# The passes with the low halves of the weights moved to the end of their bank, in a three-layer transformer kernel

## The chip, the cores and the metric

The kernel runs on one core of one Trainium2 chip. The metric is device time of one execution in microseconds (us); the kernel before takes 881.45 us, the median of three runs between 879.95 and 884.21. The engines have short names in all rows below: PE is TensorE (PEld its weight loads), DVE is VectorE, ACT is ScalarE, POOL is GpSimd, and SP is SyncE, whose queue (SPq) issues the DMA transfers.

## What is computed

256 tokens of width 1024 pass through three blocks, each modulated by a vector worked out from a condition `c` (`h = rmsnorm(x) * (1 + scale) + shift`, and a gate on the way back):

```
block 1: z = h @ w_in ; split into q_lat, kv_lat, k_rope, conv_in, gates
         q = rmsnorm(q_lat) @ w_uq ; kv = rmsnorm(kv_lat) @ w_ukv ; rope ; causal attention @ w_o_attn
         conv = silu(layernorm(causal depthwise conv, 31 taps, of a gated half)) @ w_conv_out
         x += gate1 * ((g_attn * attn + g_conv * conv) @ w_out)
         x += gate2 * mixture of experts(h2), 4 groups x 8 experts, 2 experts of one group per token
layer A: gated delta rule: 4-tap conv on q, k, v ; chunks of 64 tokens, a triangular inverse in each ;
         state scan over the chunks ; rmsnorm(o) * silu(z) @ a_w_out
layer B: forgetting attention: 16 heads of 64, decay from a cumulated log gate ; * silu(z) @ b_w_out
```

All inputs and outputs are fp32.

## The kernel before, in words

**One weight product.** [...] The activation is split into a high and a low half once per block (`split`: `h_hi` or `h4h` on ACT, `h_lo` or `h4l` on DVE, L700 and L703). Each weight piece (1 MB: 1024 rows by 256 columns, or another shape of that size) is split when it arrives (`wpieces`): the transfer fills a tile `raw` (4 buffers, from SP's queue), ACT writes the high half into a tile `hl` (L309), and `lo = raw - hi` goes into a second tile `hl` (L313). The four `hl` tiles hold two pieces. A piece is split in two halves of 128x1024 (k 0 to 3 and k 4 to 7): for the first half `lo` runs on DVE, for the second on POOL (both on POOL in a short stretch of layer A). Both engines do nothing else for that time, and everything queued behind on them waits.

**A job.** A product of one piece is a `Job`: its `load` part issues the transfer and yields the split steps, its `body` part issues 48 matmuls into one PSUM bank (2 halves of the output by 8 k by 3 passes): high weight by high activation, high weight by low activation, low weight by high activation. What they are called depends on which operand is loaded into the array:

- `gemm_feat_g` (the weight is loaded, output transposed): L483, L484, and L485 with the low half of the weight
- `gemm_tok_g` (the activation is loaded): L351, L352 with the low half of the weight, L353
- `gemm_wide`: L391, L392 (low half), L393
- `gemm_tok_m`: L424, L425 (low half), L426
- `gemm_parts`: the last product of the kernel, which has the same three passes and is not touched

The body yields after every dozen or so matmuls with its estimated cost. A feeder (`Feed`) uses these yields: it issues split steps of the next jobs, transposes, the condition products (L530, with the sums at L563 and L587 and the DVE steps L589 and L590 behind them), and pieces of the side work (the convolution's taps L1050, attention). So the order of instructions on each engine is set when the program is written out, by these yields; on the chip every engine runs its own list in order and waits at semaphores.

**Where it stands.** Block 1 runs to 284 us (attention and the convolution beside the weight products of `w_in`, then `w_o_attn`, `w_conv_out`, `w_out`), the experts to 390 us, layer A to 705 us, layer B to 884 us.

Of the kernel before, what the change touches and what calls it, by code (L numbers as in the profile page):

```python
# [179 lines left out]
class Kern:  # L180
# [146 lines left out]
    def gemm_tok_g(self, h, ko, w2d, n0, n, evac, psum=None):  # L327

        st = {}

        def load():
            st["pc"], todo = self.wpieces(w2d, 0, ko, n0, n)
            return todo

        def body():
            nc, pieces = self.nc, st["pc"]
            hh, hl = h
            if n <= 256:
                p = self.pmm()
                pts = [p[:, :n], p[:, 256:256 + n]]  # L340
                order = [(t, pc) for t in range(2) for pc in pieces]
            else:
                pts = [(psum or self.pmm)()[:, :n] for _ in range(2)]
                order = [(t, pc) for pc in pieces for t in range(2)]
            cost = 0.0
            for t, (k0, kn, whi, wlo) in order:
                for k in range(kn):
                    kk = k0 + k
                    a = hh[:, kk, t * 128:(t + 1) * 128]
                    b = hl[:, kk, t * 128:(t + 1) * 128]  # L350
                    nc.tensor.matmul(pts[t], a, whi[:, k, :], start=kk == 0, stop=False)  # L351
                    nc.tensor.matmul(pts[t], a, wlo[:, k, :], start=False, stop=False)  # L352
                    nc.tensor.matmul(pts[t], b, whi[:, k, :], start=False, stop=kk == ko - 1)  # L353
                    cost += 3 * n / 2400.0
                    if cost > 1.2:
                        yield cost
                        cost = 0.0
            with self.tc.high_priority(offset=self.LEAD):
                if n <= 256:
                    evac(p.rearrange("p (t n) -> p t n", t=2)[:, :, :n])  # L360
                else:
                    for t in range(2):
                        evac(t, pts[t])
            yield cost

        return Job(load, body)

    def gemm_wide(self, h, ko, w2d, n0, evac, n=256, step=8):

        pts = []  # L370

        def make(ka, kb):
            st = {}

            def load():
                st["pc"], todo = self.wpieces(w2d, ka, kb, n0, n)
                return todo

            def body():
                nc = self.nc  # L380
                if ka == 0:
                    pts.extend([self.pmm()[:, :n], self.ptp()[:, :n]])
                hh, hl = h
                (k0, kn, whi, wlo), = st["pc"]
                cost = 0.0
                for t in range(2):
                    for k in range(kn):
                        kk = k0 + k
                        a = hh[:, kk, t * 128:(t + 1) * 128]
                        b = hl[:, kk, t * 128:(t + 1) * 128]  # L390
                        nc.tensor.matmul(pts[t], a, whi[:, k, :], start=kk == 0, stop=False)  # L391
                        nc.tensor.matmul(pts[t], a, wlo[:, k, :], start=False, stop=False)  # L392
                        nc.tensor.matmul(pts[t], b, whi[:, k, :], start=False, stop=kk == ko - 1)  # L393
                        cost += 3 * n / 2400.0
                        if cost > 1.2:
                            yield cost
                            cost = 0.0
                    if kb == ko:
                        evac(t, pts[t])
                yield cost  # L400

            return Job(load, body)

        return [make(k, min(k + step, ko)) for k in range(0, ko, step)]

    def gemm_tok_m(self, h, ko, w2d, n0, n, evac, i0, hl=None):

        st = {}

        def load():  # L410
            st["pc"], todo = self.wpieces(w2d, 0, ko, n0, n, hl)
            return todo

        def body():
            (_, _, whi, wlo), = st["pc"]
            hh, hl_ = h
            for i in range(n // 256):
                p = self.pmm().rearrange("p (t n) -> p t n", t=2)
                sl = slice(256 * i, 256 * i + 256)
                for t in range(2):  # L420
                    for k in range(ko):
                        a, b = [o[:, k, t * 128:(t + 1) * 128] for o in (hh, hl_)]
                        mm = self.nc.tensor.matmul
                        mm(p[:, t], a, whi[:, k, sl], start=k == 0, stop=False)  # L424
                        mm(p[:, t], a, wlo[:, k, sl], start=False, stop=False)  # L425
                        mm(p[:, t], b, whi[:, k, sl], start=False, stop=k == ko - 1)  # L426
                evac(i0 + i, p)
                yield 0.64 * ko

        return Job(load, body)  # L430
# [32 lines left out]
    def gemm_feat_g(self, h, ko, w2d, n0, n, evac):  # L463

        st = {}

        def load():
            st["pc"], todo = self.wpieces(w2d, 0, ko, n0, n)
            return todo

        def body():
            nc, pieces = self.nc, st["pc"]
            hh, hl = h
            cost = 0.0
            for bp in range(n // 256):
                p = self.pmm().rearrange("p (b t) -> p b t", b=2)
                for b in range(2):
                    c0 = bp * 256 + b * 128
                    for k0, kn, whi, wlo in pieces:
                        for k in range(kn):  # L480
                            kk = k0 + k
                            wa, wb = whi[:, k, c0:c0 + 128], wlo[:, k, c0:c0 + 128]
                            nc.tensor.matmul(p[:, b, :], wa, hh[:, kk, :], start=kk == 0, stop=False)  # L483
                            nc.tensor.matmul(p[:, b, :], wa, hl[:, kk, :], start=False, stop=False)  # L484
                            nc.tensor.matmul(p[:, b, :], wb, hh[:, kk, :], start=False, stop=kk == ko - 1)  # L485
                            cost += 0.32
                            if cost > 1.2:
                                yield cost
                                cost = 0.0
                with self.tc.high_priority(offset=self.LEAD):  # L490
                    evac(bp, p)
            yield cost

        return Job(load, body)


# [2275 lines left out]
```

## Time and profile before

| | |
|---|---|
| median of three runs | 881.45 us (879.95 to 884.21) |
| the profiled execution | 885.71 us |
| its span on the core | 883.8 us |
| mean granted clock of TensorE | 0.96 of full |
| PE busy | 781.9 us, 88% of the span, 6583 matmuls |
| DVE busy | 580.1 us, 66% |
| ACT busy | 394.7 us, 45% |
| POOL busy | 284.1 us, 32% |
| memory read | 187.91 MB, 214 GB/s over the span |

The profile is of one execution, 4.3 us longer than the median of the three timed runs; 1.9 us of its time lie outside the span. Busy shares are means over stages with different limits. The rows further down come from five views: the page's summary; the list of waits, by the line that waits and what released it; the chain of work that ended last, followed back from the end; the timeline of one engine, with the idle time before an instruction and its releaser in brackets; and a table by windows of time. In names such as `hl<-raw,hl` the written tile comes first, then those read.

### The profile page before, as it was taken

The numbers are of one execution on the slowest core, as the hardware profiler recorded it, in microseconds if no ns is written. First come the engines' busy times: TensorE is split into PE (matmuls) and PEld (weight loads), VectorE is DVE, ScalarE is ACT, GpSimd is POOL, SyncE is SP. The second block draws the span as 40 slices with busy tenths as digits, with TensorE's granted clock in tenths as the row PEclk, the third lists the DMA queues.
The fourth block names the chain that finished last, engine by engine and source line by source line (L and its number), as shares of the span: only waits on it lengthen the run. The fifth ranks groups of instructions, "written<-read, shape, count | busy, mean of one in ns | idle before, by whom it ended". The sixth has DMA issues, their size and how long they took to land.

```text
span 883.8 us, 16485 instructions
## 1 busy us (share of the span) xinstructions
PE 781.9 (88%) x6583; PEld 677.2 (77%) x6583; DVE 580.1 (66%) x1167; ACT 394.7 (45%) x734; POOL 284.1 (32%) x217
## 2 busy tenths in 40 slices
PE   3779797889998899969889797998999998999996
PEld 1568676677987655538789696898998887999986
DVE  1587866675665854548778988477756466577555
ACT  2355424345544232237574235454454463554552
POOL 0144212212333200003552264134553443545433
PEclk9899999999999999999899898899999998999999
DMA  8886675777999699996444285363348643454201
GB/s 284 290 250 216 209 237 189 259 260 264 371 402 372 248 409 407 409 379 201 135 154 128 88 269 187 101 188 96 112 151 301 198 150 108 132 148 139 96 25 48
DMA packets 126325, 190.25 MB, mean 215 GB/s; under 512 B 11242, under 2 KB 84184, under 8 KB 126244
## 3 DMA queue, kind: packets, MB, share of 16 engines
q1 hardware_dynamic: 123764, 185.78, 61.0%
q10 hardware_dynamic: 1984, 1.79, 0.6%
q0 software_dynamic: 496, 1.59, 0.5%
q8 instruction: 53, 0.87, 0.4%
q14 instruction: 28, 0.23, 0.1%
HBM read 187.91 MB, written 1.22 MB: 214 GB/s over the span
## 4 chain that ended last, share of the span: by engine, by line
PE 45%; DVE 24%; DMA 15%; ACT 6%; issue 5%; POOL 3%; SPq 1%; ACTq 0%; POOLq 0%; DVEq 0%
DMA ew<-in_expert_w_up_dram 6%; DMA raw<-in_w_in_dram 6%; PE mm L351 4%; PE mm L353 4%; PE mm L352 4%; PE mm L483 3%; DVE hl L313 3%; PE mm L485 3%; PE mm L484 3%; DVE cacc L2035 2%; DVE tp L1050 2%; POOL hl L313 2%; PE mm L530 2%; ACT hl L309 2%; DMA ew<-in_expert_w_down_dram 1%
## 5 line engine op out<-in xcount | busy, mean ns | idle before, releaser
L313 POOL TENSOR_TENSOR hl<-raw,hl 128x1024 fp32r<-128x1024 f32 (+3 forms) x82 | 192.5, 2349 | 325.0 <-ACT hl L309 300.8
L309 ACT ACTIVATE hl<-raw 128x1024 fp32r<-128x1024 f32 (+4 forms) x156 | 153.7, 1018 | 50.0 <-DMA raw<-in_w_in_dram 31.1
L313 DVE TENSOR_TENSOR hl<-raw,hl 128x1024 fp32r<-128x1024 f32 (+2 forms) x74 | 99.2, 1340 | 73.0 <-ACT hl L309 72.6
L483 PE MATMUL mm<-h_hi,hl 128*128 128x256 f32 x448 | 134.4, 300 | 5.5 <-DVE b L589 2.5
L485 PE MATMUL mm<-h_hi,hl 128*128 128x256 f32 x448 | 128.8, 288 | 7.7 <-POOL hl L313 4.0
L484 PE MATMUL mm<-h_lo,hl 128*128 128x256 f32 x448 | 128.2, 286 | 0.3 <-DVE h_lo L703 0.2
L483 PEld LDWEIGHTS mm<-h_hi,hl 128*128 128x128 f32 x448 | 87.5, 195 | 10.9 <-ACT hl L309 4.1
L485 PEld LDWEIGHTS mm<-h_hi,hl 128*128 128x128 f32 x448 | 87.6, 196 | 9.5 <-POOL hl L313 5.3
L484 PEld LDWEIGHTS mm<-h_lo,hl 128*128 128x128 f32 x448 | 87.8, 196 | 1.0 <-DVE h_lo L703 0.9
L351 PE MATMUL mm<-hl,h4h 128*128 128x256 f32 (+1 forms) x256 | 76.3, 298 | 1.1 <-ACT h4h L700 0.7
L352 PE MATMUL mm<-hl,h4h 128*128 128x256 f32 (+1 forms) x256 | 72.6, 283 | 0.8 <-DVE hl L313 0.5
L353 PE MATMUL mm<-hl,h4l 128*128 128x256 f32 (+1 forms) x256 | 72.8, 284 | 0.4 <-DVE h4l L703 0.2
L1050 DVE SCALAR_TENSOR_TENSOR tp<-uq,convw,tp 128x256 f32<-128x256 f32 x120 | 58.5, 487 | 3.1
L351 PEld LDWEIGHTS mm<-hl,h4h 128*128 128x128 f32 x256 | 49.1, 192 | 2.8 <-ACT h4h L700 0.9
L352 PEld LDWEIGHTS mm<-hl,h4h 128*128 128x128 f32 x256 | 49.1, 192 | 1.2 <-DVE hl L313 0.7
L353 PEld LDWEIGHTS mm<-hl,h4l 128*128 128x128 f32 x256 | 48.8, 191 | 1.0 <-DVE h4l L703 1.0
L2035 DVE SCALAR_TENSOR_TENSOR cacc<-mm,aconv,cacc 128x255 f32<-128x255 f32 (+2 forms) x96 | 38.7, 472 | 14.0 <-ACT cacc L2032 14.0
L1332 PE MATMUL tp<-ew,xs 128*32 128x256 f32 x528 | 37.7, 379 | 4.5 <-DMA ew<-in_expert_w_up_dram 4.5
L351 PE MATMUL mm<-hl,h_hi 128*128 128x256 f32 x128 | 38.4, 300 | 0.0
L1332 PEld LDWEIGHTS tp<-ew,xs 128*32 128x32 f32 x528 | 23.1, 110 | 20.0 <-issue 9.3
L352 PE MATMUL mm<-hl,h_hi 128*128 128x256 f32 x128 | 36.4, 284 | 0.0
L353 PE MATMUL mm<-hl,h_lo 128*128 128x256 f32 x128 | 36.3, 283 | 0.0
(679 smaller groups left out, 1997.4 us busy)
## 6 DMA issues: line engine op xcount, KB each, us to landing
raw<-in_ada_w_dram SPq DMA_DIRECT2D x30, 1024.0 KB
raw<-in_a_w_in_dram SPq DMA_DIRECT2D x24, 1024.0 KB
ew<-in_expert_w_gate_dram SPq DMA_DIRECT2D x32, 512.0 KB
ew<-in_expert_w_up_dram SPq DMA_DIRECT2D x32, 512.0 KB
ew<-in_expert_w_down_dram SPq DMA_DIRECT2D x16, 1024.0 KB
raw<-in_b_w_in_dram SPq DMA_DIRECT2D x15, 1024.0 KB
raw<-in_w_in_dram SPq DMA_DIRECT2D x12, 1024.0 KB
raw<-in_a_w_out_dram SPq DMA_DIRECT2D x8, 1024.0 KB
```

What stands on the lines that cost most here:

```text
L309: nc.scalar.activation(pc[2][:, ks], v[:, ks], AF.Copy)
L313: eng.tensor_tensor(pc[3][:, ks], v[:, ks], pc[2][:, ks].bitcast(F), OP.subtract)
L351: nc.tensor.matmul(pts[t], a, whi[:, k, :], start=kk == 0, stop=False)
L352: nc.tensor.matmul(pts[t], a, wlo[:, k, :], start=False, stop=False)
L353: nc.tensor.matmul(pts[t], b, whi[:, k, :], start=False, stop=kk == ko - 1)
L483: nc.tensor.matmul(p[:, b, :], wa, hh[:, kk, :], start=kk == 0, stop=False)
L484: nc.tensor.matmul(p[:, b, :], wa, hl[:, kk, :], start=False, stop=False)
L485: nc.tensor.matmul(p[:, b, :], wb, hh[:, kk, :], start=False, stop=kk == ko - 1)
L530: nc.tensor.matmul(p[32 * g:32 * g + 32, :], crep[:, hf * 4 + g, :], raws[hf][:, g, :], start=hf == 0, stop=hf == 1)
L1050: nc.vector.scalar_tensor_tensor(dst, u[:, b, tp:tp + 256], w(b, tp), dst, op0=OP.mult, op1=OP.add)
L1332: nc.tensor.matmul(pg[32 * s:32 * s + 32, :], xs[:, k, c0 + 32 * s:c0 + 32 * s + 32], gu[s][:, :, k * 128:(k + 1) * 128], start=k == 0, st ...
L2035: nc.vector.scalar_tensor_tensor(acc[:, b, sh:], p[:, b, 0:256 - sh], w(b, 3 - sh), acc[:, b, sh:], op0=OP.mult, op1=OP.add)
```

## The change

In the four functions named above the passes that use the low half of the weight are issued after all passes with the high half, for both halves of the output. A bank now takes 32 matmuls with the high half (high and low activation in turn), then 16 with the low half. The count of matmuls, their operands and their weight loads stay as they are. The bank is cleared once (`start` on its first matmul only) and closed once, because the two output halves are now both open at the same time. `gemm_wide` hands over its first bank only when the low passes of that bank are through, eight matmuls before the end of the job, where it used to do so at the job's half. The cost that a matmul reports to the feeder is nearly the same, so the yields come again after about a dozen matmuls. Lines behind the changed functions move by 10 (L687 is L697 in the new numbering, L587 is L597, L530 is L540, L600 is L610, L1116 is L1126); in the changed functions L483, L484, L485 become L494, L495, L492, and L351, L352, L353 become L356, L353, L357.

```diff
 # gemm_feat_g (gemm_tok_g, gemm_wide and gemm_tok_m are rewritten in the same way)
-                for b in range(2):
+                for late, b in ((0, 0), (0, 1), (1, 0), (1, 1)):
                     c0 = bp * 256 + b * 128
                     for k0, kn, whi, wlo in pieces:
                         for k in range(kn):
                             kk = k0 + k
                             wa, wb = whi[:, k, c0:c0 + 128], wlo[:, k, c0:c0 + 128]
-                            nc.tensor.matmul(p[:, b, :], wa, hh[:, kk, :], start=kk == 0, stop=False)
-                            nc.tensor.matmul(p[:, b, :], wa, hl[:, kk, :], start=False, stop=False)
-                            nc.tensor.matmul(p[:, b, :], wb, hh[:, kk, :], start=False, stop=kk == ko - 1)
-                            cost += 0.32
+                            if late:
+                                nc.tensor.matmul(p[:, b, :], wb, hh[:, kk, :], start=False, stop=kk == ko - 1 and b == 1)
+                            else:
+                                nc.tensor.matmul(p[:, b, :], wa, hh[:, kk, :], start=kk + b == 0, stop=False)
+                                nc.tensor.matmul(p[:, b, :], wa, hl[:, kk, :], start=False, stop=False)
+                            cost += 0.11 if late else 0.21
 # gemm_wide
-                for t in range(2):
+                for late, t in ((0, 0), (0, 1), (1, 0), (1, 1)):
...
-                    if kb == ko:
+                    if late and kb == ko:
                         evac(t, pts[t])
```

The transposes of the q latent (`qn`) and of the kv latent (`kn`) on PE, in block 1 at 59 to 70 us. Before, the q transposes stand after 36 matmuls of the first gate product, and those of the kv latent after the 12 left of it and 12 of the next:

```order
L485 MATMUL mm<-h_hi,hl 128x256
L687 MATMUL tp<-ident,qn 128x128 x6
L483 MATMUL mm<-h_hi,hl 128x256
L484 MATMUL mm<-h_lo,hl 128x256
L485 MATMUL mm<-h_hi,hl 128x256
```

And now, after 32 matmuls with the high half, of which the last four rows are shown:

```order
L494 MATMUL mm<-h_hi,hl 128x256
L495 MATMUL mm<-h_lo,hl 128x256
L494 MATMUL mm<-h_hi,hl 128x256
L495 MATMUL mm<-h_lo,hl 128x256
L492 MATMUL mm<-h_hi,hl 128x256 x4
L697 MATMUL tp<-ident,qn 128x128 x6
L492 MATMUL mm<-h_hi,hl 128x256 x12
L494 MATMUL mm<-h_hi,hl 128x256
```

The transposes stand at the same place, after 36 matmuls; the low half of the first piece is met for the first time four matmuls ahead of them, where it used to be the third matmul of the job.

The start of the first convolution product on PE at 234 us (`u` is the convolution's output, `ah` and `al` the attention's, L587 a sum for the condition). Before:

```order
L485 MATMUL mm<-ah,hl 128x256
L483 MATMUL mm<-u_hi,hl 128x256
L484 MATMUL mm<-u_lo,hl 128x256
L485 MATMUL mm<-u_hi,hl 128x256
```

Twelve such rows on, L587 follows:

```order
L485 MATMUL mm<-u_hi,hl 128x256
L587 MATMUL mm<-ident,finr 128x16
L483 MATMUL mm<-u_hi,hl 128x256
L484 MATMUL mm<-u_lo,hl 128x256
L485 MATMUL mm<-u_hi,hl 128x256
```

And now:

```order
L492 MATMUL mm<-ah,hl 128x256 x8
L597 MATMUL mm<-ident,finr 128x16
L494 MATMUL mm<-u_hi,hl 128x256
L495 MATMUL mm<-u_lo,hl 128x256
L494 MATMUL mm<-u_hi,hl 128x256
L495 MATMUL mm<-u_lo,hl 128x256
```

L587 has moved ahead of the product, and it no longer stands behind a matmul that needs a low half of that product's weights.

On DVE at the same place the two steps behind that sum (L589, L590) move up by one (`gates` are the block's gates, `mod` the modulation). Before:

```order
L313 TENSOR_TENSOR hl<-raw,hl 128x1024
L1116 TENSOR_TENSOR gates_1236<-mm,gates_1236 128x512 x2
L589 TENSOR_REDUCE mod_425<-mm 128x4
L590 TENSOR_TENSOR mod_425<-mod_425,adab 128x4
L313 TENSOR_TENSOR hl<-raw,hl 128x1024
```

And now:

```order
L313 TENSOR_TENSOR hl<-raw,hl 128x1024
L1126 TENSOR_TENSOR gates_1235<-mm,gates_1235 128x512
L599 TENSOR_REDUCE mod_425<-mm 128x4
L600 TENSOR_TENSOR mod_425<-mod_425,adab 128x4
L1126 TENSOR_TENSOR gates_1235<-mm,gates_1235 128x512
L313 TENSOR_TENSOR hl<-raw,hl 128x1024
```

One gate step trades places with them; the split of the next weight piece (L313) keeps its place behind both.

The first product with `w_out` on PE at 250 us (`yh` and `yl` are the two halves of its activation, which DVE and ACT finish in four pieces of two k each while the product runs). Now, its end:

```order
L356 MATMUL mm<-hl,yh 128x256
L357 MATMUL mm<-hl,yl 128x256
L353 MATMUL mm<-hl,yh 128x256 x16
```

Before, each k of it had its three matmuls in a row; now the 16 that need only `yh` and the low half of the weight come behind the last that needs `yl`. The orders of POOL and SP are the same before and after; ACT's has a few neighbours that trade places.

## Rows read from the trace of the kernel before

**Rows 1.** The page: busy time by engine, and the chain that ended last by engine.

```profile
PE 781.9 (88%) x6583; PEld 677.2 (77%) x6583; DVE 580.1 (66%) x1167; ACT 394.7 (45%) x734; POOL 284.1 (32%) x217
...
PE 45%; DVE 24%; DMA 15%; ACT 6%; issue 5%; POOL 3%; SPq 1%; ACTq 0%; POOLq 0%; DVEq 0%
```

**Rows 2.** Waits, weight loads on PE (line, releaser: us in total, times, longest).

```profile
PEld mm L485 <- POOL hl L313: 6.5, 7, 1.9
...
PEld mm L485 <- DVE hl L313: 4.3, 3, 2.5
...
PEld mm L425 <- DVE hl L313: 1.7, 1, 1.7
...
PEld mm L392 <- POOL hl L313: 1.2, 1, 1.2
```

**Rows 3.** The chain, 60 to 83 us (start us, us, what).

```profile
60.40 2.39 POOL hl L313
...
62.84 0.39 PE mm L485
...
69.18 0.44 PE tp L687 x4
...
80.47 1.06 ACT hl L309
...
81.55 1.23 DVE hl L313
```

**Rows 4.** Timeline, 60 to 68 us (start us, us, what, idle before and releaser).

```profile
60.33 0.38 PE L485 MATMUL mm<-h_hi,hl 128*128 128x256 f32 x1 [0.76 <-DVE hl L313]
...
64.76 2.38 POOL L313 TENSOR_TENSOR hl<-raw,hl 128x1024 fp32r<-128x1024 f32 x1
...
64.83 2.47 DVE L985 TENSOR_SCALAR kn<-kvl,rstd 128x256 f32<-128x256 f32 x1 [0.49 <-POOL rstd L618]
```

**Rows 5.** Windows: us, busy by engine (instructions), clock, DMA share, GB/s.

```profile
81.00:117.00 36.00, 28.57 (x217) 24.96 (x210) 32.68 (x58) 14.29 (x24) 13.75 (x8) 0.95 0.56 181
110.13:113.54 3.41, 3.21 (x15) 3.21 (x16) 3.23 (x8) 1.24 (x2) 2.04 (x1) 0.50 0.57 178
740.00:830.00 90.00, 89.67 (x735) 87.72 (x735) 60.05 (x101) 45.41 (x96) 43.04 (x24) 0.97 0.43 136
```

**Rows 6.** Timeline of DVE, 93 to 111 us.

```profile
93.86 2.49 DVE L313 TENSOR_TENSOR hl<-raw,hl 128x1024 fp32r<-128x1024 f32 x1
...
106.88 3.39 DVE L313 TENSOR_TENSOR hl<-raw,hl 128x1024 fp32r<-128x1024 f32 x1
```

**Rows 7.** The chain, 124 to 138 us.

```profile
124.35 8.14 DMA raw<-in_w_in_dram
...
135.23 2.33 POOL hl L313
```

**Rows 8.** Timeline of POOL and DVE, 246 to 250 us.

```profile
246.63 2.41 POOL L313 TENSOR_TENSOR hl<-raw,hl 128x1024 fp32r<-128x1024 f32 x1 [8.08 <-ACT hl L309]
...
246.92 2.13 DVE L590 TENSOR_TENSOR mod<-mod,adab 128x4 f32<-128x4 f32 x1
```

**Rows 9.** Timeline of PE, 236 to 255 us.

```profile
236.09 0.39 PE L485 MATMUL mm<-u_hi,hl 128*128 128x256 f32 x1 [1.07 <-POOL hl L313]
...
254.54 0.39 PE L353 MATMUL mm<-hl,yl 128*128 128x256 f32 x1 [0.23 <-DVE yl L1127]
```

**Rows 10.** Timeline of PE, 447 to 454 us.

```profile
447.51 0.38 PE L485 MATMUL mm<-h_hi,hl 128*128 128x256 f32 x1 [1.73 <-POOL hl L313]
...
452.50 1.05 PE L2103 MATMUL tp<-ones,vt 128*128 128x1 f32 x8 [0.47 <-ACT vt L2097]
```

**Rows 11.** Timeline of PE in layer B, 709 to 768 us.

```profile
709.80 0.39 PE L353 MATMUL mm<-hl,h4l 128*128 128x256 f32 x1 [0.23 <-DVE h4l L703]
...
739.80 0.42 PE L1248 MATMUL tp<-ident,qa 128*66 128x128 f32 x1 [3.73 <-DVE qa L2636]
...
767.03 0.39 PE L352 MATMUL mm<-hl,h4h 128*128 128x256 f32 x1 [0.33 <-POOL hl L313]
```

More of the change, by code (lines that the diff above doesn't have):

```diff
@@ L340, in body @@
                 pts = [p[:, :n], p[:, 256:256 + n]]
-                order = [(t, pc) for t in range(2) for pc in pieces]
             else:
                 pts = [(psum or self.pmm)()[:, :n] for _ in range(2)]
-                order = [(t, pc) for pc in pieces for t in range(2)]
             cost = 0.0
[L346 to L357, printed above, removed]
+            for late in (False, True):
+                for t, (k0, kn, whi, wlo) in [(t, pc) for t in range(2) for pc in pieces]:
+                    for k in range(kn):
+                        kk = k0 + k
+                        a = hh[:, kk, t * 128:(t + 1) * 128]
+                        b = hl[:, kk, t * 128:(t + 1) * 128]
+                        if late:
+                            nc.tensor.matmul(pts[t], a, wlo[:, k, :], start=False,
+                                             stop=kk == ko - 1 and (t == 1 or n > 256))
+                        else:
+                            nc.tensor.matmul(pts[t], a, whi[:, k, :], start=kk == 0 and (t == 0 or n > 256), stop=False)
+                            nc.tensor.matmul(pts[t], b, whi[:, k, :], start=False, stop=False)
+                        cost += (1 if late else 2) * n / 2400.0
+                        if cost > 1.2:
+                            yield cost
+                            cost = 0.0
             with self.tc.high_priority(offset=self.LEAD):
@@ L390, in body @@
                         b = hl[:, kk, t * 128:(t + 1) * 128]
[L391 to L394, printed above, removed]
+                        if late:
+                            nc.tensor.matmul(pts[t], a, wlo[:, k, :], start=False, stop=kk == ko - 1)
+                        else:
+                            nc.tensor.matmul(pts[t], a, whi[:, k, :], start=kk == 0, stop=False)
+                            nc.tensor.matmul(pts[t], b, whi[:, k, :], start=False, stop=False)
+                        cost += (1 if late else 2) * n / 2400.0
                         if cost > 1.2:
@@ L419, in body @@
                 sl = slice(256 * i, 256 * i + 256)
-                for t in range(2):
+                mm = self.nc.tensor.matmul
+                for late, t in ((0, 0), (0, 1), (1, 0), (1, 1)):
                     for k in range(ko):
                         a, b = [o[:, k, t * 128:(t + 1) * 128] for o in (hh, hl_)]
[L423 to L426, printed above, removed]
+                        if late:
+                            mm(p[:, t], a, wlo[:, k, sl], start=False, stop=k == ko - 1 and t == 1)
+                        else:
+                            mm(p[:, t], a, whi[:, k, sl], start=k + t == 0, stop=False)
+                            mm(p[:, t], b, whi[:, k, sl], start=False, stop=False)
                 evac(i0 + i, p)
@@ L482, in body @@
                             wa, wb = whi[:, k, c0:c0 + 128], wlo[:, k, c0:c0 + 128]
-                            nc.tensor.matmul(p[:, b, :], wa, hh[:, kk, :], start=kk == 0, stop=False)
-                            nc.tensor.matmul(p[:, b, :], wa, hl[:, kk, :], start=False, stop=False)
-                            nc.tensor.matmul(p[:, b, :], wb, hh[:, kk, :], start=False, stop=kk == ko - 1)
-                            cost += 0.32
+                            if late:
+                                nc.tensor.matmul(p[:, b, :], wb, hh[:, kk, :], start=False, stop=kk == ko - 1 and b == 1)
+                            else:
+                                nc.tensor.matmul(p[:, b, :], wa, hh[:, kk, :], start=kk + b == 0, stop=False)
+                                nc.tensor.matmul(p[:, b, :], wa, hl[:, kk, :], start=False, stop=False)
+                            cost += 0.11 if late else 0.21
                             if cost > 1.2:
```

## The prediction

> **What bounds the kernel now.** I read the summary first, then the list of waits, then the chain stage by stage, and last the timeline around each wait. The summary shows PE busy for 88% of the span, while the chain that ended last gives PE only 45%, DVE 24% and DMA 15% [rows 1]. So about half of the chain lies on other engines: PE's long stretches bound layers A and B, and in block 1 the chain goes through splits, convolution taps and transfers. That matters here, because the change touches PE alone. It takes no work from any engine and issues every matmul with the same operands.
>
> The list of waits names what the change can remove: the weight loads of the low passes wait for a low half 6.5 + 4.3 + 1.7 + 1.2 = 13.7 us in all [rows 2]; smaller groups left out bring it to some 15. That is 1.7% of the span. A wait removed on PE counts only if what follows it on the chain was waiting for PE, so I went through them by place.
>
> **The change part by part.** A matmul costs 90 us / 735 = 0.12 us in a dense stretch [rows 5]. Their count does not change, so 6583 of them cost what they did: 0. In a bank the first low pass used to be the second or third matmul and becomes number 33, so it is reached about 30 x 0.12 = 3.6 us after the job's start. A POOL split takes 2.33 to 2.41 us [rows 3, 7, 8], so it is then usually done.
>
> *60 to 82 us, the first gate product and the transposes.* Here the chain runs through the change: POOL's split 60.40 to 62.79, then L485 at 62.84, then dense PE work up to the high split at 80.47 and DVE's low split at 81.55 [rows 3]. PE waits twice in this job, 0.76 us idle at 60.33 [rows 4] and again before 62.84, some 2.2 us counted from matmul to matmul. If both go, PE reaches the transposes of `kn` at about 67.0 in place of 69.18 [rows 3]. But DVE writes `kn` from 64.83 to 67.30 [rows 4], so this becomes the next wait: they start at about 67.4, a gain of 1.8. The next product but one then meets its own low half early and gives back an estimated 0.3. I take -1.5, with bounds 0 (if DVE's or POOL's order holds it) and -2.2 (both stalls). It is handed on by the high split at 80.47, which waits for PE here.
>
> *81 to 117 us.* PE has its longest waits here, four of them, two being the longest of their rows, 2.5 and 1.9 us [rows 2]. But DVE is busy 32.68 of 36.00 us [rows 5], with taps, rotary steps and the low splits themselves. The chain stays on DVE throughout; PE waits for a split that DVE would not make any earlier. I take 0. The cover is DVE's queue; without it the four waits would be worth about 6 us, the lower bound. [...]
>
> [...]
>
> *117 to 213 us.* The chain is transfer, high split, low split, buffer free, next transfer: 8.14 us for one transfer and 2.33 for POOL [rows 7], and so on for six transfers. No pass of PE stands in it. I take 0: the stage only starts 1.5 us earlier. Bounds 0 to -0.5, since a buffer `hl` freed by PE is nowhere the last thing waited for in it.
>
> *213 to 284 us.* At 236.09 L485 waits 1.07 us for POOL [rows 9]; this wait goes, and L587 moves ahead of the product. But DVE's steps L589 and L590 behind it run into POOL's splits either way: at 246.92 the tiny L590 takes 2.13 us, up to the end of the split of 246.63 + 2.41 = 249.04 [rows 8]. The gate steps and `yl` follow on DVE, and the `w_out` product waits for the last `yl` at 254.54 [rows 9]. In that product the order now costs: while PE waits for `yl`, the low passes of the pieces at hand used to fill the time. When the last piece comes, 28 of 48 matmuls are left before and 35 after: 7 x 0.12 = +0.8. PE is dense to the end of the stage, so this is paid. The same holds for the first product with `wo`, for which I take +0.2 (two matmuls). Bounds: +1.0 as summed, and -0.1 if the 1.07 us of the wait at 236.09 do reach the end.
>
> *390 to 538 us.* The wait at 447.51 is the largest single one here, 1.73 us idle [rows 10]. The next thing that PE needs is `vt` from ACT at 452.50, where it waits again [rows 10], so that wait grows by what is saved. I take 0, bounds 0 to -2.0. The first product of layer A starts on pieces of `h_lo`, as `w_out` does on `yl`: up to +0.8, which ACT's and DVE's later work covers: 0.
>
> *538 to 705 us.* Two waits of about 0.3 us with PE dense around them: -0.6; bounds 0 to -0.6. `gemm_wide`'s first bank is handed over later; the evacuation runs beside the other bank's last eight matmuls (about 1 us), so 0, bounded by +0.3 for the last of them.
>
> *Layer B.* Its first product waits for `h4l` at 709.80 [rows 11]; +0.8 on PE. PE then waits 3.73 us for DVE's `qa` at 739.80 [rows 11], which covers it: 0. The wait at 767.03, 0.33 us idle and some 0.6 counted from matmul to matmul, lies in a stretch where PE is busy 89.67 of 90.00 us [rows 5, 11], so it counts: -0.6. The last product is not changed: 0.
>
> *The sum.* -1.5 + 0.8 + 0.2 - 0.6 - 0.6 = -1.7 us. The profiled execution took 885.71, so by its own time 884.0. The median of the runs shown is 881.45, 4.3 us lower. Taken from that, 879.7 us, or 0.2% less.
>
> **The rivals.**
>
> *The waits count in full.* If most of the waits removed reach the end (DVE and POOL then get their inputs earlier and shift too), the gain is 10 to 15 us: 866 to 872. For it: the chain carries low splits in all stages, the wait at 62.84 among them [rows 3]. Against it: the largest ones lie where DVE or a transfer is the chain [rows 5, 7]. A middle case (81 to 117 in part) gives 5 us, 876. Chance 0.24 for a gain above 4.4 us.
>
> *Slower: the low passes were the filler, and the splits collide.* Where a product starts on activations that arrive piece by piece (`yl`, `h_lo`, `h4l`, `al`), each costs up to 0.8 us: four places, 3.2 us. Where PE comes earlier, it frees `hl` earlier, so POOL's split starts earlier and falls beside DVE work it used to miss: a low split on DVE takes 2.49 or 3.39 us beside POOL's [rows 6] and 1.23 alone [rows 3], so 1.3 to 2.2 us each time. With the gain at 60 us gone as well, three such hits give 3.2 + 3 x 1.7 = 8 us at the most, 5.5 in the middle: 887. It decides when DVE's queue is on the chain where they fall, as from 81 to 117 us. Against it: the order on POOL and SP is the same as before, and in the stage after 117 us the transfers set the pace. Chance 0.16.
>
> [...]
>
> *Nothing reaches the end.* The wait for `kn` stays where it was, and the rest is covered: 881.5. Chance 0.17; the forecast itself has 0.43.
>
> **How the numbers follow.** About 0.5% (4.4 us) is what a measurement of this kernel can tell from no change. The forecast and "nothing" both lie within it: 0.43 + 0.17 = 0.60. Faster 0.24, slower 0.16. The likeliest case alone has a range of 877 to 883, from the bounds of its terms and the spread of the runs shown. The whole range reaches into the gains to 869 and into the slower case to 887; about 1 in 10 is left out on either side.
>
> **What would show it.** In the changed profile the waits of the low passes for L313 should fall from some 14 us to under 3, while PE's waits for ACT's and DVE's other work grow. The transposes of `kn` should stand at 67 to 68 us behind DVE's `kn`; DVE's window from 81 to 117 should start 1.5 us earlier and have the same length; the `w_out` product should end about 0.8 us later after the last `yl`. The forecast is wrong if the stage from 81 to 117 gets shorter by over 2 us (the first rival), or if DVE's low splits take longer in more places than before (the second).

## The result: 0.6% slower, and the profile after

The changed kernel takes 887.81 us, the median of 8 runs, where the kernel before takes 880.84 in the same rounds: a ratio of 1.0064 (95% interval 1.0043 to 1.0085). A second set of runs gave 1.0051 (1.0032 to 1.0071). The profiled execution took 887.61 us, near the median; that of before, 885.71, lies 4.9 us above its median. So the two spans differ by 2.0 us only, and totals are taken from the timed runs.

The page of the changed kernel, busy times and the chain's shares, answering to [rows 1]:

```profile
PE 790.6 (89%) x6583; PEld 686.1 (77%) x6583; DVE 576.2 (65%) x1167; ACT 395.0 (45%) x734; POOL 288.3 (33%) x217
...
PE 50%; DVE 21%; DMA 13%; ACT 6%; issue 6%; POOL 3%; SPq 0%; ACTq 0%; POOLq 0%; DVEq 0%
```

PE is busy 8.7 us longer with the same 6583 matmuls, and holds more of the chain. The waits of its weight loads for low halves, answering to [rows 2]:

```profile
PEld mm L431 <- DVE hl L313: 2.9, 1, 2.9
...
PEld mm L431 <- POOL hl L313: 0.3, 1, 0.3
```

13.7 us have become 3.2: the change does what it says. 2.9 us of the rest are one wait of `gemm_tok_m` (L431, which was L425), which has grown from 1.7. The timeline at the transposes of `kn`, answering to [rows 3, 4]:

```profile
65.49 2.48 DVE L995 TENSOR_SCALAR kn<-kvl,rstd 128x256 f32<-128x256 f32 x1 [0.48 <-POOL rstd L628]
...
67.92 0.66 PE L697 MATMUL tp<-ident,kn 128*128 128x128 f32 x4
```

They now start when DVE has written `kn`, as forecast. The largest loss is in layer A. The timeline of PE and ACT there, answering to [rows 10] (L2113 was L2103, L2042 was L2032, the evacuation of a product's bank):

```profile
452.23 1.53 PE L492 MATMUL mm<-h_hi,hl 128*128 128x256 f32 x11
...
456.49 1.86 PE L2113 MATMUL tp<-ones,vt 128*128 128x1 f32 x8 [2.72 <-ACT vt L2107]
...
458.21 0.56 PE L492 MATMUL mm<-h_hi,hl 128*128 128x256 f32 x1
...
458.81 0.84 ACT L2042 ACTIVATE cacc<-mm,aconv 128x256 f32<-128x256 f32 x2 [2.07 <-PE mm L492]
```

Two things are to be seen. The wait at 447 us is gone, and the wait for `vt` has grown from 0.47 to 2.72 us. And L2113 stands behind the 47th matmul of the product, not behind its 48th: the last one, at 458.21, comes after the wait, and ACT waits 2.07 us for it before it can evacuate the bank. Windows by time, first of the changed kernel, behind this wait; then of the kernel before, in the same length from its own L2103 on (columns as in [rows 5]):

```profile
453.00:456.10 3.10, 0.77 (x7) 0.57 (x6) 3.10 (x4) 2.45 (x5) 2.35 (x1) 1.00 0.90 304
456.10:462.93 6.83, 6.44 (x30) 6.44 (x31) 4.33 (x11) 4.10 (x10) 1.25 (x1) 0.50 0.51 154
```

```profile
452.50:459.33 6.83, 6.83 (x61) 6.83 (x61) 6.35 (x17) 4.38 (x10) 2.41 (x1) 1.00 0.53 156
```

After the longer wait the clock is granted at 0.50 for 6.83 us: 30 matmuls start where 61 did, and PE is busy for 6.44 us of it. From DVE's split L313 ahead of this place to L2223 (now L2233), which needs what comes out of it, the traces of before and after say (timeline of DVE, one fence each):

```profile
440.92 1.96 DVE L313 TENSOR_TENSOR hl<-raw,hl 128x1024 fp32r<-128x1024 f32 x1
...
465.40 2.34 DVE L2223 TENSOR_TENSOR Mt<-At,tp 128x1024 f32<-128x1024 f32 x2
```

```profile
444.90 1.69 DVE L313 TENSOR_TENSOR hl<-raw,hl 128x1024 fp32r<-128x1024 f32 x1
...
473.40 1.21 DVE L2233 TENSOR_TENSOR Mt<-At,tp 128x1024 f32<-128x1024 f32 x1
```

24.48 us before, 28.50 after: 4.0 us lost in a stage for which the prediction had 0.

### The profile page after: what moved, and what is told of

It is laid out like the page before. It is cut to its first block, busy times and chain, and to the rows that moved or that the text cites. A ratio compares the mean times of both kernels' runs of the same rounds, so it can differ in the third digit from the quotient of the medians.

```text
span 885.8 us, 16482 instructions
## 1 busy us (share of the span) xinstructions
PE 790.6 (89%) x6583; PEld 686.1 (77%) x6583; DVE 576.2 (65%) x1167; ACT 395.0 (45%) x734; POOL 288.3 (33%) x217
## 4 chain that ended last, share of the span: by engine, by line
PE 50%; DVE 21%; DMA 13%; ACT 6%; issue 6%; POOL 3%; SPq 0%; ACTq 0%; POOLq 0%; DVEq 0%
DMA ew<-in_expert_w_up_dram 6%; PE mm L353 5%; PE mm L356 5%; PE mm L357 5%; DMA raw<-in_w_in_dram 4%; PE mm L492 4%; PE mm L494 3%; PE mm L495 3%; DVE tp L1060 2%; PE mm L540 2%; DVE hl L313 2%; DVE cacc L2045 2%; DMA ew<-in_expert_w_down_dram 2%; DMA raw<-in_a_w_in_dram 1%; PE tp L2460 1%
## 5 line engine op out<-in xcount | busy, mean ns | idle before, releaser
L313 POOL TENSOR_TENSOR hl<-raw,hl 128x1024 fp32r<-128x1024 f32 (+3 forms) x82 | 196.2, 2396 | 321.5 <-ACT hl L309 268.7
L313 DVE TENSOR_TENSOR hl<-raw,hl 128x1024 fp32r<-128x1024 f32 (+2 forms) x74 | 102.7, 1387 | 68.2 <-ACT hl L309 64.5
L494 PE MATMUL mm<-h_hi,hl 128*128 128x256 f32 x448 | 117.4, 299 | 5.5 <-DVE b L599 2.3
L495 PE MATMUL mm<-h_lo,hl 128*128 128x256 f32 x448 | 113.0, 290 | 0.6 <-DVE h_lo L713 0.6
L494 PEld LDWEIGHTS mm<-h_hi,hl 128*128 128x128 f32 x448 | 89.5, 200 | 10.6 <-ACT hl L309 4.1
L495 PEld LDWEIGHTS mm<-h_lo,hl 128*128 128x128 f32 x448 | 89.4, 200 | 1.2 <-DVE h_lo L713 1.2
L356 PE MATMUL mm<-hl,h4h 128*128 128x256 f32 (+1 forms) x256 | 66.2, 294 | 0.7 <-ACT h4h L710 0.7
L492 PE MATMUL mm<-h_hi,hl 128*128 128x256 f32 x448 | 66.7, 290 | 0.0
L357 PE MATMUL mm<-hl,h4l 128*128 128x256 f32 (+1 forms) x256 | 63.6, 284 | 1.0 <-DVE h4l L713 1.0
L492 PEld LDWEIGHTS mm<-h_hi,hl 128*128 128x128 f32 x448 | 57.8, 193 | 0.8
L356 PEld LDWEIGHTS mm<-hl,h4h 128*128 128x128 f32 x256 | 49.0, 191 | 2.0 <-ACT h4h L710 0.9
L357 PEld LDWEIGHTS mm<-hl,h4l 128*128 128x128 f32 x256 | 49.0, 192 | 1.8 <-DVE h4l L713 1.8
L353 PE MATMUL mm<-hl,h4h 128*128 128x256 f32 (+1 forms) x256 | 35.3, 283 | 0.0
L356 PE MATMUL mm<-hl,h_hi 128*128 128x256 f32 x128 | 32.7, 294 | 0.0
L353 PEld LDWEIGHTS mm<-hl,h4h 128*128 128x128 f32 x256 | 32.0, 188 | 0.4
L540 PE MATMUL mm<-raw,crep 128*32 128x512 f32 x240 | 31.7, 650 | 0.1
L357 PE MATMUL mm<-hl,h_lo 128*128 128x256 f32 x128 | 31.6, 285 | 0.0
```

Of the source, the lines that this page charges most:

```text
L313: eng.tensor_tensor(pc[3][:, ks], v[:, ks], pc[2][:, ks].bitcast(F), OP.subtract)
L356: nc.tensor.matmul(pts[t], a, whi[:, k, :], start=kk == 0 and (t == 0 or n > 256), stop=False)
L494: nc.tensor.matmul(p[:, b, :], wa, hh[:, kk, :], start=kk + b == 0, stop=False)
L540: nc.tensor.matmul(p[32 * g:32 * g + 32, :], crep[:, hf * 4 + g, :], raws[hf][:, g, :], start=hf == 0, stop=hf == 1)
```

## The experiments

Three theories. A: the yield one matmul short of the bank's end lets waiting work in ahead of the last matmul. B: products that start on activations in pieces have lost the filler. C: short waits have merged into longer ones, behind which the clock is granted at half. All ratios are to the kernel before, run in the same rounds; they differ a little from the quotients of the medians given beside them.

**Which function, and which theory.** The first kernel changes two numbers, so that the yields come after 12, 24, 36 and 48 matmuls again:

```diff
-                            cost += 0.11 if late else 0.21
+                            cost += 0.32 / 3 if late else 0.64 / 3
```

> The changed kernel with one edit: in gemm_feat_g a pair of high passes reports 0.64/3 and a low pass 0.32/3 us of cost (0.21 and 0.11 before), so that the fourth yield of a bank comes after its 48th matmul and not after its 47th. Theory A (the yield one matmul short of the end puts transposes that wait, such as L2113 for vt at 456 us, ahead of the bank's last matmul, and the evacuation waits for them): most of the loss of 7 us against before goes, 879 to 883 us. Theory B (the products that start on activations arriving in pieces have lost their filler): 887 to 888 as the changed kernel, nothing gained. Theory C (PE's waits are now longer ones, after which the clock is granted at half more often): 885 to 888, with the mean granted clock still near 0.95.

Measured: 884.01 us, 1.0021 (0.9994 to 1.0048). About 3 us of the loss went (2.6 to 3.8, by which of the changed kernel's two ratios is taken), as A says, though its 879 to 883 us are just missed; not all of the loss went, and the intervals overlap.

The second is the kernel before, unchanged.

> The kernel before, unchanged, for the granted clock of each of its runs and a second trace. Theory C: the clock of its runs lies above that of the changed kernel's (0.932 to 0.960, mean 0.948), at 0.960 or higher. Theories A and B: the clock ranges overlap, and 883 us shows no other difference than the scatter of runs, 879 to 884.

Measured: 884.18 us, 1.0019 (0.9998 to 1.0040), which shows how far scatter alone reaches. Its mean clock over 12 runs is 0.956, that of the changed kernel 0.948. That is the direction of C, but C had put it at 0.960 or higher, and the ranges overlap, as A and B had it: this run decides nothing between them.

The third and fourth split the change by function.

```diff
 # in words, not code. third: the kernel before, with this exchange; fourth: the kernel after, with the opposite one
-    gemm_feat_g of before
+    gemm_feat_g of after
```

> The new order in gemm_feat_g alone, the other three functions as before. Theory A: the whole loss is there, 887 to 888 us. Theory B: the loss is shared, since w_out and layer B go through gemm_tok_g; 883 to 885. Theory C: in proportion to the waits removed, which are mostly in this function: 885 to 888.

> The new order in gemm_tok_g, gemm_wide and gemm_tok_m, and gemm_feat_g as before. Theory A: no loss, 879 to 882 us. Theory B: half the loss, about 884. Theory C: few waits are changed, 880 to 882.

Measured: 1.0042 (1.0013 to 1.0070) with `gemm_feat_g` alone, 1.0019 (1.0002 to 1.0036) without it, the same as the unchanged kernel. By the medians, 888.18 against 883.73 us, the loss is in `gemm_feat_g`; the intervals overlap, but one stage of the traces, in the table further down, shows it too. B's "about 884" for the fourth kernel is met in number only, since the unchanged kernel took 884.18 beside it.

**Yield and order apart.** The changed kernel once more, and the kernel before with only the yield's place moved:

```diff
 # gemm_feat_g of before
+                            if ko == 8 and b and kk == 7:
+                                yield cost + 0.21
+                                cost = -0.21
                             nc.tensor.matmul(p[:, b, :], wb, hh[:, kk, :], start=False, stop=kk == ko - 1)
```

> The changed kernel again, as it is, on the chip of the three runs beside it. All theories: 1.004 to 1.008 of before, 887 to 889 us on a chip where before takes 882 to 883.

> The kernel before with its own order of passes; only the fourth yield of a bank in gemm_feat_g (8 k) comes after the 47th matmul in place of the 48th. Theory A (the yield's place is the loss): 1.003 to 1.005 of before, some 3 to 4 us slower. Theory C (merged waits and the clock behind them): 1.000 to 1.002, since every wait for a low half stays where it was.

Measured: 886.56 us, 1.0051, for the first; 885.44 us, 1.0034 (1.0003 to 1.0064), for the second. The yield's place alone seems to cost time in the old order too, as A says. The total is weak evidence for it: the interval begins hardly above 1, the unchanged kernel reached 1.0019, and the runs spread from 879.95 to 892.87. The trace says it more clearly (table further down).

**The old order at one place.** The mended kernel with the old passes in layer A, then in the `w_out` products as well:

```diff
-            return self.gemm_feat_g(h, 8, win, 1024 * a + 256 * i, 256, ev)
+            return self.gemm_feat_g_o(h, 8, win, 1024 * a + 256 * i, 256, ev)
 # and the v products; the second kernel also:
-            return self.gemm_tok_g((yh, yl), 8, inp["w_out"][0], 256 * i, 256, ev)
+            return self.gemm_tok_g_o((yh, yl), 8, inp["w_out"][0], 256 * i, 256, ev)
```

> The changed kernel with the fourth yield mended as in the first experiment, and the old order of passes in the eight q/k and eight v products of layer A (gemm_feat_g there), so that PE again meets the POOL split at 447 us in the middle of a product. Theory C: PE's wait for vt at about 453 us falls from 2.4 us to about 0.5, the half clock behind it goes, and the stage from 441 to 465 us takes 24.5 us as before and not 27.5; 1.000 or below, 2 to 3 us less than the first experiment's 1.002. Theory A alone: no difference to the first experiment.

> As the kernel beside it, and the four products with w_out in the old order too (it starts on activations that arrive in pieces). Theory B: another 0.6 us less than beside it, seen between the last yl and L565 behind the first product, 254 to 259 us. Theory C: the same as beside it, since no wait for a low half is in these products; 0.998 to 1.000 of before in all, about 881 to 882.

Measured: 1.0025 (1.0005 to 1.0045) and 1.0024 (1.0005 to 1.0044). In the first one's timeline of DVE the stage is as C expects:

```profile
441.28 1.97 DVE L313 TENSOR_TENSOR hl<-raw,hl 128x1024 fp32r<-128x1024 f32 x1
...
465.75 2.34 DVE L2266 TENSOR_TENSOR Mt<-At,tp 128x1024 f32<-128x1024 f32 x2
```

24.47 us, the wait for `vt` 0.49. But neither total fell below the mended kernel's 1.0021, where C had 1.000 or below and 0.998 to 1.000, nor is B's 0.6 us to be seen between the two: misses, and why the totals did not fall is open.

**The clock by itself.** The kernel before with the new order (yield mended) in layer A only; and the mended kernel with 18 extra matmuls in the wait for `vt`:

```diff
             def sums():
+                for _ in range(18 if (a, i) == (0, 3) else 0):
+                    nc.tensor.matmul(full[a][:, 256:512], h[0][:, 0, 0:128], h[0][:, 0, :], start=True, stop=True)
```

> The kernel before with one change: the new order (its fourth yield behind the 48th matmul) in layer A's q/k and v products alone. Theory C: PE's wait before L2103 at about 453 us grows from 0.5 to 2.4 us or more, half clock behind it, and the stage from 441 to 465 us takes 27.5 us in place of 24.5; 1.002 to 1.004 of before. Theory A alone (only the yield's place costs): 24.5 us there and 1.000 to 1.002.

> The first experiment's kernel (new order, yield mended) with 18 extra matmuls, whose result nobody reads, ahead of L2113 for the fourth q product, so that PE computes for about 2 us of its wait for vt at 453 us. Theory C with the clock as the price: no half clock behind this wait, and the time from the convolution step at 454 us to L2223 at 465 us, 13.5 us in the first experiment and 11.3 before, falls back to 11.3 to 11.7. If the price is the order and not the clock: it stays at 13.5 or grows by what the extra matmuls take. In all 0 to 2 us less than the first experiment.

> The kernel before, unchanged, a second time: how far a run under another name lies from the shared runs of before on this chip. All theories: 0.998 to 1.002.

> The first experiment's kernel again, on the chip of the three beside it. Theory A: 1.000 to 1.002, equal to the unchanged kernel within the interval; Theory C: 1.002 to 1.003, and again a wait of 2.4 us at 453 us with half clock behind it.

Measured, in this order: 1.0006 (0.9985 to 1.0027), 0.9990 (0.9970 to 1.0010), 1.0003 (0.9983 to 1.0024), 1.0025 (1.0004 to 1.0047). The timeline of PE and the window behind the wait, first with the extra matmuls, then without them:

```profile
453.72 2.32 PE L2111 MATMUL tp<-h_hi 128*128 128x256 f32 x18
...
456.30:463.13 6.83, 6.83 (x59) 6.83 (x59) 6.35 (x17) 4.19 (x10) 2.42 (x1) 1.00 0.50 156
```

```profile
455.69 1.87 PE L2113 MATMUL tp<-ones,vt 128*128 128x1 f32 x8 [2.39 <-ACT vt L2107]
...
455.36:462.19 6.83, 6.50 (x30) 6.50 (x31) 5.49 (x17) 4.53 (x10) 2.38 (x1) 0.50 0.51 154
```

And DVE's stage in both:

```profile
444.68 1.97 DVE L313 TENSOR_TENSOR hl<-raw,hl 128x1024 fp32r<-128x1024 f32 x1
...
469.36 2.34 DVE L2236 TENSOR_TENSOR Mt<-At,tp 128x1024 f32<-128x1024 f32 x2
```

```profile
444.10 1.97 DVE L313 TENSOR_TENSOR hl<-raw,hl 128x1024 fp32r<-128x1024 f32 x1
...
471.74 2.34 DVE L2233 TENSOR_TENSOR Mt<-At,tp 128x1024 f32<-128x1024 f32 x2
```

Useless work of 2.3 us shortens the stage from 27.64 to 24.68 us: the same instructions behind the wait run at a clock of 1.00 in place of 0.50, and 59 matmuls start where 30 did. So the price of the merged wait is the clock, not the order. In total it is 884.38 against 881.41 us, 3.0 less on one chip. With the new order in layer A alone the stage takes 27.68 us (DVE L313 at 441.94, the line that was L2223 at 469.62), yet its total of 1.0006 is not clearly above the unchanged kernel's 1.0003, and C's 1.002 to 1.004 is missed. The stage's 3 us are shown in all six traces with the new order there and no extra matmuls; how much of it reaches the end is shown by one pair (3.0) and not by two others (about 0 each).

**Where the yield costs.** The kernel with the extra matmuls, again and in three variants: `w_out` in the old order; the yield behind the 47th matmul in block 1 only; in layer A only.

```diff
 # in the products of block 1, or in those of layer A
-                            cost += 0.32 / 3 if late else 0.64 / 3
+                            cost += 0.11 if late else 0.21
```

> The kernel of the extra matmuls (new order, yield mended, PE kept busy before the fourth q product's L2113), with the four products of w_out in the old order. Forecast's own term: 0.6 us less than that kernel, between the last yl and L565 (253.8 to 258.9 us), 0.997 to 0.999 of before, 880 to 881 us. Rival: the old order meets half clock there as often, and no difference can be seen, 0.999 to 1.000.

> The kernel of the extra matmuls, with the fourth yield behind the 47th matmul again in block 1's five gemm_feat_g places, and behind the 48th in layer A. If the yield's loss lies in block 1 (224 to 232 us, where the changed kernel lost 1.3): 1.001 to 1.002 of before. If it lies in layer A: 0.999, as the kernel of the extra matmuls.

> The kernel of the extra matmuls, with the fourth yield behind the 47th matmul again in layer A's q/k and v products, and behind the 48th in block 1. If the loss lies in layer A (one matmul of the third q product behind L2113, the evacuation after it): 1.001 to 1.003 of before, and 25.3 us or more from 441 to 465 us in place of 24.7. If it lies in block 1: 0.999.

> The kernel of the extra matmuls again, on the chip of the three beside it. Theory A and C together (the yield and the clock are the whole loss): 0.997 to 1.001 of before, as the first time.

Measured: 1.0001 (0.9975 to 1.0027), 0.9972 (0.9952 to 0.9992), 1.0034 (1.0008 to 1.0061), and 1.0004 (0.9986 to 1.0022) for the repeat. The old order in `w_out` gains nothing that the total could show, as its rival said. The yield's loss lies in layer A: 885.24 against 882.48 us, and the stage from DVE's split at 445 to L2223 takes 25.9 us in place of 24.5 to 24.7. One place of it on PE, with the window behind it: the transposes of `kq` with the yield at 47 in layer A, then in the kernel that has it at 48 there and at 47 in block 1.

```profile
469.71 2.83 PE L2267 MATMUL tp<-kq 128*128 128x128 f32 x12 [1.99 <-ACT kq L2085]
...
469.85:473.26 3.41, 3.41 (x17) 3.41 (x18) 2.83 (x3) 0.73 (x3) 0.00 (x0) 0.50 0.35 94
```

```profile
467.89 1.60 PE L2267 MATMUL tp<-kq 128*128 128x128 f32 x12 [0.68 <-ACT kq L2085]
...
469.85:473.26 3.41, 3.41 (x33) 3.41 (x32) 1.91 (x3) 0.98 (x3) 0.00 (x0) 1.00 0.78 258
```

The evacuation behind the late 48th matmul makes `kq` late, the wait grows from 0.68 to 1.99 us, and half clock follows (0.50 for 3.41 us, where it is 1.00 with the shorter wait): 17 matmuls in place of 33. (This profiled execution took 893.89 us, far above the kernel's median; the place is read from it and not the total.) In block 1 the yield at 47 does not cost, and seems to gain: 0.9972 is less than either theory gave.

**The version that beats both.** The yield at 47 in block 1 and at 48 in layer A, with the extra matmuls, again, and with the old order in `w_out`:

```diff
-            return self.gemm_tok_g((yh, yl), 8, inp["w_out"][0], 256 * i, 256, ev)
+            return self.gemm_tok_g_o((yh, yl), 8, inp["w_out"][0], 256 * i, 256, ev)
```

> The kernel with the yield behind the 47th matmul in block 1 and behind the 48th in layer A (and the extra matmuls), with the four products of w_out in the old order as well. If the forecast's filler term holds by itself: 0.6 us less than the kernel beside it, 0.996 to 0.998 of before. If half clock in that stage hides it: the same as beside it.

> The kernel with the yield behind the 47th matmul in block 1 and behind the 48th in layer A again. If its 0.9972 was a real gain: 0.996 to 0.999 of before; if it was the scatter of runs: 0.999 to 1.001.

Measured: 879.75 us, 0.9962 (0.9939 to 0.9984), with `w_out` in the old order, and 880.62 us, 0.9969 (0.9947 to 0.9991), for the repeat, where before takes 883.13. With the 0.9972 of the first time, all three lie below 1 with their whole interval, by 0.3 to 0.4%, and all three were measured on one chip. Against the changed kernel it is 0.8 to 1.0%, by ratios from different rounds. Between the changed kernel and the repeat lie two edits in layer A: two numbers of a cost, and 18 matmuls that compute nothing.

The filler term of `w_out` can be read by itself: DVE's last `yl` and L565, which follows the product, in the kernel before; in the unchanged kernel's second trace, with half clock in this stage; in the changed kernel, with half clock too; and in the last version with the old order, without:

```profile
253.80 0.69 DVE L1127 TENSOR_TENSOR yl<-yt,yh 128x512 fp32r<-128x512 f32 x1 [0.69 <-ACT yh L1126]
...
258.93 0.16 DVE L565 TENSOR_TENSOR mod<-mm,adab 128x4 f32<-128x4 f32 x1 [2.48 <-PE mm L563]
```

```profile
253.06 0.69 DVE L1127 TENSOR_TENSOR yl<-yt,yh 128x512 fp32r<-128x512 f32 x1 [0.69 <-ACT yh L1126]
...
259.73 0.16 DVE L565 TENSOR_TENSOR mod<-mm,adab 128x4 f32<-128x4 f32 x1 [4.01 <-PE mm L563]
```

```profile
254.56 0.69 DVE L1137 TENSOR_TENSOR yl<-yt,yh 128x512 fp32r<-128x512 f32 x1 [0.70 <-ACT yh L1136]
...
261.77 0.16 DVE L575 TENSOR_TENSOR mod<-mm,adab 128x4 f32<-128x4 f32 x1 [4.56 <-PE mm L573]
```

```profile
252.09 0.69 DVE L1213 TENSOR_TENSOR yl<-yt,yh 128x512 fp32r<-128x512 f32 x1 [0.70 <-ACT yh L1212]
...
257.23 0.16 DVE L651 TENSOR_TENSOR mod<-mm,adab 128x4 f32<-128x4 f32 x1 [2.48 <-PE mm L649]
```

Old order: 5.13 and 5.14 us at full clock (1.00 from 253.80 to 260.60 in the kernel before), 6.67 with half clock for a part. New order: 7.21 with half clock for the same length (0.50 for 3.41 us, 254.71 to 258.12). So the order costs 0.5 us at equal clock, and the half clock 1.5. The same two rows in all 20 traces agree: the old order takes 5.0 to 5.1 us without half clock and 6.7 with 3.41 us of it, the new order 7.2 to 7.5 with 3.41 us. None of the 11 traces with the new order is without half clock here, and 4 of the 9 with the old order are; that the order brings the half clock is suggested by this, not shown. In totals the filler is not told apart: 0.9962 against 0.9969.

**One stage in all 20 traces.** In every trace DVE makes the split that stands at 441 us in the kernel before and, six splits later, the one that stands at 498, so the time between the two can be compared without the scatter of the rest. In the kernel before it ends with

```profile
497.70 1.22 DVE L313 TENSOR_TENSOR hl<-raw,hl 128x1024 fp32r<-128x1024 f32 x1
```

and in the changed kernel (its start at 444.90 is shown above) with

```profile
505.68 1.22 DVE L313 TENSOR_TENSOR hl<-raw,hl 128x1024 fp32r<-128x1024 f32 x1
```

The new order with the yield mended (first experiment), the old order with the yield at 47, and the extra matmuls with the yield at 47 in layer A:

```profile
441.39 1.97 DVE L313 TENSOR_TENSOR hl<-raw,hl 128x1024 fp32r<-128x1024 f32 x1
...
500.30 1.22 DVE L313 TENSOR_TENSOR hl<-raw,hl 128x1024 fp32r<-128x1024 f32 x1
```

```profile
440.70 1.70 DVE L313 TENSOR_TENSOR hl<-raw,hl 128x1024 fp32r<-128x1024 f32 x1
...
500.79 1.23 DVE L313 TENSOR_TENSOR hl<-raw,hl 128x1024 fp32r<-128x1024 f32 x1
```

```profile
445.02 1.71 DVE L313 TENSOR_TENSOR hl<-raw,hl 128x1024 fp32r<-128x1024 f32 x1
...
506.06 1.22 DVE L313 TENSOR_TENSOR hl<-raw,hl 128x1024 fp32r<-128x1024 f32 x1
```

| layer A's q, k and v products | traces | split at 441 to L2223, us | split at 441 to split at 498, us |
|---|---|---|---|
| old order, yield at 48 | 6 | 24.5 to 24.7 | 56.8 to 56.9 |
| new order, yield at 48 | 3 | 27.5 to 27.7 | 58.9 to 59.0 |
| old order, yield at 47 | 1 | 25.7 | 60.1 |
| new order, yield at 47 (the change) | 3 | 28.2 to 28.5 | 60.5 to 60.8 |
| new order, yield at 48, extra matmuls | 6 | 24.5 to 24.7 | 56.8 to 56.9 |
| new order, yield at 47, extra matmuls | 1 | 25.9 | 61.0 |

The kernel with the new order in `gemm_feat_g` alone is one of the three with the change, the one without it one of the six of the first row. Of the merged wait's 3.0 us, 2.1 to 2.2 are left at 498; the yield alone costs 3.2 to 4.2 there, and both together 3.7 to 4.0, so the two prices do not add up. Behind 498 the traces scatter by up to 4.6 us until 575, with and without the change, and no total is to be split up more finely than that.

## Why the prediction was wrong, point by point

- *The waits removed*: 13.7 to 3.2 us, where under 3 was written. Right.
- *60 to 82 us*, forecast -1.5: right in its mechanism, `kn` the next wait. From DVE's first rotary step (62.92 before) to the split of 81.55 it takes 17.59 us where it took 18.63: -1.0. With `gemm_feat_g` alone in the new order it takes 18.30, with the three other functions alone 18.45, so the gain needs both, and not only the first gate product that the prediction named.
- *81 to 117 us*, forecast 0: from the split of 81.55 to that of 116.25, 34.7 us before and 35.1 after (34.8 and 35.5 in two more traces of the unchanged kernel). DVE's queue covered the waits. The 1.9 us counted among the waits here is the one at 447; the second longest here is the 1.7 of L425.
- *117 to 213 us*, forecast 0: from the split of 116.25 to that of 202.50, 86.3 to 85.8 us, and 84.0 and 85.3 in the two other traces of the unchanged kernel. No change is to be seen; but the chain does hold passes of PE, from 173.6 to 177.5, where the prediction had none.
- *213 to 284 us*, forecast +0.8 at `w_out`: +0.5 at equal clock. The mechanism holds, but the stage was mis-sized: from the split of 202.50 to that of 262.26 it takes 59.8, 61.6 and 61.6 us in three traces of the unchanged kernel and 62.8 and 63.0 in two of the changed one. The half clock in it, 1.5 us at `w_out` alone, was no term of the sum.
- *390 to 538 us*, forecast 0 with bounds 0 to -2.0: **this step failed**. "So that wait grows by what is saved" was right, and it was priced at nothing. The wait grew from 0.47 to 2.4 or 2.7 us, and behind it the clock was granted at 0.50 for 6.83 us in a stretch where PE sets the pace: +3.0 us in the stage, shown by taking away the half clock alone, and 2.1 to 2.2 us of it still there at 498. The bound had no end above zero, though [rows 5, 6] showed 0.50 for 3.41 us behind a stall of PE (`110.33 0.58 PE L485 MATMUL mm<-h_hi,hl 128*128 128x256 f32 x1 [2.30 <-DVE hl L313]`); the sum had no term for it.
- *The yields*: front and prediction took the reported cost as "nearly the same". The sum 11 x 0.11 = 1.21 passes the limit of 1.2 one matmul early, so the fourth yield fell to the 47th. This cost had no term in the sum. It adds 0.8 us between the split at 441 and the convolution at 454 (14.8 with it, 14.0 with the yield mended), 3.2 to 4.2 us by the split at 498 where it stands without the merged wait, and some 3 us in all by three pairs of totals, each pair alone at the edge of its interval.
- *538 to 705 us*, forecast -0.6: from the split of 540.7 to that of 697.8, 157.1, 154.7 and 154.1 us in three traces of the unchanged kernel, 152.0 and 153.4 in two of the changed one. Faster, and by more than was said; half clock comes and goes in this stretch (behind the wait for `zb`, 0.50 from 667.30 to 668.50 us before and 1.00 from 669.00 to 672.41 after), so the term itself can't be told.
- *Layer B*, forecast -0.6: from one `qkT` evacuation at 744.8 to the next at 773.8, 28.0 us after and 28.6 to 29.0 before. Right.
- *The sum without the two causes*: 0.9990 and 1.0004, where the forecast said 0.998. So the gain of 1.7 us is not shown either.
- *The rival on the slower side*: its 887 lies beside the measured 887.8 by luck. Its filler part is borne out, by 0.5 to 0.8 us at `w_out`. Of its splits that collide there is little: DVE's low splits of over 1.5 us are 11 and 12 in two traces of the changed kernel and 9, 10 and 9 in three of the unchanged one, none of the new ones between 81 and 117 us, and two of the faster kernels (0.9990 and 0.9969) have 10 and 11. Its largest case was also added up low: 3.2 + 3 x 2.2 = 9.8 us by its own prices, not 8.

## What to carry to other kernels

A wait on PE that is removed is not gone when something later holds PE: it joins the next wait, and one wait of 2.4 us cost the stage 3 us more than two of 1.7 and 0.5 because the clock behind it fell to half (0.50 for 6.83 us) where PE was needed. Before removing a wait, see what PE does after the wait that takes its place; where nothing useful can be moved there, matmuls that compute nothing can pay: here 18 of them, 2.32 us, made the stage 3.0 us shorter. And when a body is rewritten whose yields place other work, count where each yield falls, above all the last one before an evacuation.

## What the runs showed of the hardware that was not expected

Half clock (0.50) followed PE waits of 1.99 us (for `kq`), 2.39 and 2.72 us (for `vt`) and was not seen behind those of 0.24 us (for `vt`, with the extra matmuls), 0.47 and 0.49 us (for `vt`) and 0.68 us (for `kq`), nor behind the 1.73 us at 447 before (1.00 from 447.50 to 450.90); it lasted 3.41 us in some places (254.71 to 258.12 in the changed kernel) and 6.83 in others (456.10 to 462.93). It does not follow every such wait: behind the 2.10 us that PE waits for `zb` in layer A, at 666 us before and at 669 after, it came in the trace of before (0.50 from 667.30 to 668.50) and not in that of the changed kernel (1.00 from 669.00 to 672.41), and of two more traces of the unchanged kernel only one has it (matmuls of 0.41 us from 668.21 on, 0.28 elsewhere). The unchanged kernel's runs have a mean clock of 0.955 to 0.959, set by set, and the changed kernel's 0.948 and 0.950. The runs of one kernel differ by several us, and in each set of the unchanged kernel those with the lower mean clock tend to be the longer ones (correlation of clock and time -0.35 to -0.73, over seven sets of 12 to 35 runs).
